# Six instead of four SwiGLU tile pairs from seven products, with each pair's operand sums emitted in the middle of the next pair

## The chip, the cores and the metric

The kernel runs on one core of one Trainium2 chip. The metric is the device time of one execution in microseconds, as a median over runs. The engines are named as the profile names them: PE is TensorE (matmuls), PEld its weight loads, DVE VectorE, ACT ScalarE, POOL GpSimd, SP SyncE, which issues all the DMAs spoken of here.

## What is computed

A decoder block in float32 over 512 tokens of 1024 channels: two token mixers side by side, merged by gates, then a SwiGLU channel mixer with 2816 hidden channels (22 tiles of 128).

```python
D_MODEL, BATCH, SEQ, D_CONV, D_RNN = 1024, 1, 512, 1024, 1280
D_FF = ((int(math.ceil(8 * D_MODEL / 3)) + 255) // 256) * 256      # 2816

h = rmsnorm(x, norm1_g[l])
z = h @ w_in[l] + b_in[l]
z_glu, z_rx, z_rg, z_ga, z_gb = jnp.split(z, split_idx, axis=-1)
...
y_a = u @ conv_w_out[l] + conv_b_out[l]
...
y_b = (hb * jax.nn.gelu(z_rg, approximate=True)) @ lru_w_out[l]
m = jax.nn.sigmoid(z_ga) * y_a + jax.nn.sigmoid(z_gb) * y_b
x = x + m @ w_mix_out[l]

h = rmsnorm(x, norm2_g[l])
x = x + (jax.nn.silu(h @ ffn_w1[l]) * (h @ ffn_w3[l])) @ ffn_w2[l]
return rmsnorm(x, norm_f_g)
```

## The kernel before

**Numbers in two parts.** TensorE multiplies float32 values rounded to a shorter form (F32R), so every factor is held as a high part and the rest, and a product is three matmuls: high by high, high by low, low by high (`mm3` for whole tiles, `Sevenfold.product` for quarters). Making the two parts is a "split": a copy on ACT (L117) and a subtraction (L113) on DVE, or on POOL for the first weights.

**Weights come in blocks.** `wchunk` lists them in the order of use, `emit_chunk` issues one: a DMA of 512 KB into one of four raw buffers (L144, or L242 for the output weights), then the split into one of five hl buffers. `weights` emits four blocks ahead of the one asked for. Blocks carry names: f1_6 is tile 6 of `ffn_w1`, fb11_4 and ft2_4 (here "fb", "ft") blocks for pair 4 from seven products, ob11_2, ob21_2, ot2_0 and so on those of the output weights `ffn_w2`.

**Stages.** TensorE goes through the input product (z), the two mixer outputs (yb with the lo blocks, ya with the co blocks), the mixer's output matrix (mxr), the SwiGLU (f, fr), the last product (or), in this order. An instruction scheduler orders the instructions on each engine by their emission and readiness; some places are fixed by `issue_after`.

**Products of quarters.** A matrix product whose factors are cut into 2x2 quarters can be made with seven quarter products in place of eight, from sums of quarters. `Quartered` and `Sevenfold` do it for `w_mix_out` and `ffn_w2`: `make_sums` loads two 512 KB rows of quarters (ows, L279), makes four sums with four DVE operations of 128x512 and stores them in DRAM as four pieces of 256 KB (ot, L289), from where they are loaded as weights; `Sevenfold.pair` makes the sums of the other factor for one k (ous, s1, s1p, oe, ov); `run` multiplies them, in a first loop over k with the quarters b21 and b11 and the sum t1 (blocks ob21 for two k at a time, and ob11 with b11 and t1 for each k), then in a second.

**The SwiGLU.** The 22 hidden tiles are taken as 11 pairs k = 0 to 10 (tile k and tile k + 11). A direct pair multiplies all of `h2` by the four weight blocks f1 and f3 of its two tiles, with 512 columns a matmul. The pairs in `SEVEN`, 2 to 5, come from `ffn_seven`: seven products r1 to r7 of 256 columns (its seven weight blocks include four sums of quarters), put together in `c11`, `c12`, `c21` and `q`, with `out_of` for the silu and the product with the second factor. The sums of these pairs' weights are made long before, beside the input product: `make_f_sums` is a generator, advanced once for each step of `ORDER` and once for each lo tile; each of its 16 steps loads 4 x 256 columns of `ffn_w1` or `ffn_w3` into a buffer of the pool `wsums` (fws, L334), lets POOL make four sums (128x256) and stores them (fs, L349).

**Order around the change.** After each pair, `out_sums(n)` makes the next n sets of sums of `ffn_w2`: k % 2 after a pair from seven products, two after a direct pair, all that are left after the last. Before, sets 2 and 3 stand after pairs 3 and 5, sets 4 and 5 after pair 6, 6 and 7 after pair 7, 8 and 9 after pair 8, 10 after pair 9. Behind pair 10 come the first blocks of the last product, and the loads of the residual rows x2b and of the final norm's gain gf (`loads`, 10 x 256 KB), which `run` calls after k = 0.

Of the kernel before, what the change touches and what calls it, by code (L numbers as in the profile page):

```python
# [9 lines left out]
F32R = mybir.dt.float32r  # L10
# [3 lines left out]
P = 128  # L14
T = 512
# [25 lines left out]

SEVEN = (2, 3, 4, 5)
SUMS_AT, SUMS_STEP, SUMS_LAG, STORE_LAG = 4, 3, 2, 5


# [33 lines left out]
def tile_block(ctx, tc, a, out):  # L81
    nc = tc.nc
    pool = lambda name, bufs, **k: ctx.enter_context(tc.tile_pool(name=name, bufs=bufs, **k))
    consts = pool("consts", 1)
    raws = pool("raws", RAW)
    hls = pool("hls", HL)
    wsums = pool("wsums", 3)
    psum = pool("psum", 6, space=bass.MemoryType.PSUM)
    psum2 = pool("psum2", 2, space=bass.MemoryType.PSUM)

# [6 lines left out]
    def pairt(name, dtype=F32R):  # L97

        return longt(f"{name}h", dtype), longt(f"{name}l", dtype)

    def bank(name):
        return psum.tile([P, T], F32, tag="mm", name=name)
# [4 lines left out]
    vec, act, pe, pool_e = nc.vector, nc.scalar, nc.tensor, nc.gpsimd  # L107
# [4 lines left out]
    def sub(eng, o, x, y):  # L112
        return eng.tensor_tensor(out=o, in0=x, in1=y, op=ALU.subtract)  # L113

    def split_to(h, l, full, eng, copy=act.copy):

        copy(h, full)  # L117
        last = sub(eng, l, full, h.bitcast(F32))
        if eng is pool_e:
            newest["sub"] = last.ins  # L120
        return h, l

    def split(name, full, eng, p_=None, copy=act.copy):
        p_ = p_ or pairt(name)
        return split_to(*p_, full, eng, copy)
# [4 lines left out]
    emitted = [0]  # L130
# [166 lines left out]
    F_SUMS = ("t2", "t1", "t4", "t3")  # L297
    f_sums = {k: dram.tile([P, 4, 1024], F32, tag=f"fs{k}", name=f"fs{k}") for k in SEVEN}

# [15 lines left out]
    def make_f_sums():  # L315

        todo = [(k, i, c) for k in SEVEN for i in range(2) for c in (0, 2)]
        sums_due, stores_due = [], []  # L320
        n = 0
        while todo or sums_due or stores_due:
            if stores_due and emitted[0] >= stores_due[0][0]:
                stores_due.pop(0)[1]()
            if sums_due and n >= sums_due[0][0]:
                sums_due.pop(0)[1]()
            if todo and n >= SUMS_AT and (n - SUMS_AT) % SUMS_STEP == 0:
                k, i, c = todo.pop(0)
                raw = wsums.tile([P, 1024], F32, tag="wsum", name=f"fws{k}_{i}_{c}")
                q = [raw[:, 256 * m : 256 * m + 256] for m in range(4)]  # L330
                four = (w1, w3)[i].rearrange("p (h k) (e n) -> p h k e n", h=2, e=2)
                with tc.issue_after(newest["load"]):
                    for h in range(2):
                        nc.sync.dma_start(  # L334
                            raw[:, h * T : h * T + T].rearrange("p (e k n) -> p e k n", e=2, k=2),
                            four[:, h, c : c + 2, :, k * P : (k + 1) * P].rearrange("p k e n -> p e k n"),
                        )

                def sums(raw=raw, q=q, k=k, at=T * i + P * c):
                    q11, q12, q21, q22 = q  # L340
                    with tc.issue_after(newest["sub"]):
                        sub(pool_e, q22, q22, q12)
                        sub(pool_e, q12, q12, q11)
                        pool_e.tensor_tensor(out=q11, in0=q22, in1=q11, op=ALU.add)
                        sub(pool_e, q21, q21, q11)

                    def stores():
                        with tc.issue_after(newest["load"]):
                            nc.sync.dma_start(f_sums[k][:, :, at : at + 256], raw.rearrange("p (m n) -> p m n", m=4))  # L349

                    stores_due.append((emitted[0] + STORE_LAG, stores))

                sums_due.append((n + SUMS_LAG, sums))
            n += 1
            yield

    for k in range(KF):
        if k in SEVEN:
            for n in ("b11", "b21", "b22", "t2", "t1", "t3", "t4"):
# [68 lines left out]
    def pc(name, i):  # L428
        return par[:, col[name] + i : col[name] + i + 1]
# [14 lines left out]
    def w_tiles(key, kt, ahead=AHEAD):  # L444
        h, l = weights(key, ahead)
        return [(h[:, k, :], l[:, k, :]) for k in range(kt)]
# [205 lines left out]
    def run_beside(n):  # L652
        for _ in range(n):
            next(side, None)
# [107 lines left out]
    f_sums_steps = make_f_sums()  # L762
# [30 lines left out]
            mixq.make_sums(j // 2 - 1)  # L793
    yb = sgb
    run_beside(1000)
    for _ in f_sums_steps:
        pass


    add = lambda o, x, y: vec.tensor_tensor(out=o, in0=x, in1=y, op=ALU.add)  # L800
# [8 lines left out]

    class Sevenfold:  # L810
        def __init__(self, q):
            self.q, self.uv, self.ops = q, [], []
            self.name, self.kh = q.name, q.kh

        def tile(self, j, make):

            k, i = j % self.kh, j // self.kh
            if i == 0:
                self.uv.append((longt(f"{self.name}u{k}"), longt(f"{self.name}v{k}")))
            for dst, cs in zip(self.uv[k], HALVES):  # L820
                make(cs, dst[:, HALVES[i]])
            if i:
                self.pair(k, *self.uv[k])

        def pair(self, k, ua, va):

            n = self.name
            u_ = split(f"{n}us{k}", ua, vec)
            s1 = shortt(f"{n}s1{k}")[:, LO]
            add(s1, va[:, LO], va[:, HI])  # L830
            sp = longt(f"{n}s1p{k}", F32R)
            split_to(sp[:, LO], sp[:, HI], s1, vec)
            e = longt(f"{n}e{k}")
            sub(vec, e[:, HI], ua[:, LO], va[:, LO])
            sub(vec, va[:, LO], s1, ua[:, LO])
            sub(vec, e[:, LO], ua[:, HI], va[:, LO])
            self.ops.append((u_, sp, e, va))
# [58 lines left out]
    for n, j in enumerate(mixq.order()):  # L896
        ws = w_tiles(f"co{j}", ND)
        ps = bank(f"ya{j}")
        mm3(ps, ws, un)
        o = sga[j]  # L900
        vec.scalar_tensor_tensor(out=o, in0=ps, scalar=pc("conv_b_out", j), in1=o, op0=ALU.add, op1=ALU.mult)
        m7.tile(j, lambda cs, dst: add(dst, o[:, cs], yb[j][:, cs]))
        if n == 0:
            mixq.make_sums(3)


    x2 = [[longt(f"x2{t}{h}") for h in range(2)] for t in range(NT)]
# [48 lines left out]
    o7 = Sevenfold(outq)  # L956
# [54 lines left out]
    def ffn_seven(k):  # L1011
        u_, v_ = longt(f"ou{k}"), longt(f"ov{k}")

        def product(ps, x_, w_, again=False):

            h, l = weights(f"f{w_}_{k}")
            for i in range(2):
                for c, (xh, xl) in enumerate(f_in[x_]):
                    for m, (lw, rx_) in enumerate(((h, xh), (h, xl), (l, xh))):
                        pe.matmul(  # L1020
                            ps[:, HALVES[i]], lw[:, 4 * i + c, :], rx_, start=not (again or i or c or m),
                            stop=bool(i and c == 3 and m == 2), skip_group_check=True,
                        )

        def out_of(c, dst):
            act.activation(c[:, LO], c[:, LO], AF.Silu)
            vec.tensor_tensor(out=dst, in0=c[:, LO], in1=c[:, HI], op=ALU.mult)

        r1, r2, r3, r5, r7 = bank(f"fr1_{k}"), bank2(f"fr2_{k}"), bank(f"fr3_{k}"), bank2(f"fr5_{k}"), bank(f"fr7_{k}")
        product(r1, "a11", "b11")  # L1030
        c11 = shortt(f"c11_{k}")
        act.copy(c11, r1)
        product(r2, "a12", "b21")
        add(c11, r2, c11)
        out_of(c11, u_[:, LO])
        product(r3, "s4", "b22")
        product(r1, "s2", "t2", True)
        q = shortt(f"q_{k}")
        act.copy(q, r1)
        product(r5, "s1", "t1")  # L1040
        add(q, r5, q)
        c12 = shortt(f"c12_{k}")
        add(c12, r3, q)
        out_of(c12, u_[:, HI])
        product(r7, "s3", "t3")
        c21 = shortt(f"c21_{k}")
        act.copy(c21, r7)
        add(q, r7, q)
        out_of(q, v_[:, HI])
        product(r1, "a22", "t4", True)  # L1050
        add(c21, r1, c21)
        out_of(c21, v_[:, LO])
        o7.uv.append((u_, v_))
        o7.pair(k, u_, v_)

    for k in range(1, KF):
        if k in SEVEN:
            ffn_seven(k)
            out_sums(k % 2)
            continue  # L1060
        for j in (k, k + KF):
            p1, p3 = bank(f"f1_{j}"), bank(f"f3_{j}")
            mm3(p1, w_tiles(f"f1_{j}", ND), h2)
            mm3(p3, w_tiles(f"f3_{j}", ND), h2)
            ffn_out(j, p1, p3)
        out_sums(2 if k < KF - 1 else KF)
# [96 lines left out]
```

## Time and profile before

| what | value |
|---|---|
| median of 3 runs | 814.71 us (814.35 to 815.43) |
| the profiled execution, whole | 814.89 us |
| its span | 813.0 us |
| PE busy in the span | 800.0 us |
| DVE / ACT / POOL busy | 644.1 / 443.1 / 210.3 us |
| DMA, moved / mean rate | 153.46 MB / 189 GB/s |
| granted clock of TensorE | 0.995 |

The span is what the profiler recorded from the first instruction to the last; 1.9 us of the profiled execution lie around it. Busy times are sums over instructions of one engine, so they overlap between engines. The names left of an arrow are what an instruction writes, right of it what it reads, with the buffer numbers left out: "f" are the banks of direct pairs, "fr" those of pairs from seven products, "or" those of the last product.

### The profile page before, as it was taken

The page shows a single profiled execution, that of the slowest core. Times are in us where ns is not written, and L with a number is a line of the kernel's source. Part 1 is how long each engine was busy: PE and PEld are TensorE (multiplying, and loading weights), DVE is VectorE, ACT ScalarE, POOL GpSimd, SP SyncE. Part 2 cuts the span into 40 slices and gives each one's busy share as a digit, 9 for nine tenths or more (in the row PEclk, how much of TensorE's full clock was granted, in tenths as well). Part 3 has the DMA queues.
Part 4 walks back from the last instruction along what each step waited for, and adds up shares of the span by engine and source line. Part 5 has one row for each costly group of instructions (what it writes and reads, how often), then busy time and mean ns, then how long its engine had stood idle before and what let it go on. Part 6 is the DMA issues. An engine that isn't in the chain of part 4 may idle for free.

```text
span 813.0 us, 11453 instructions
## 1 busy us (share of the span) xinstructions
PE 800.0 (98%) x4038; PEld 683.3 (84%) x4038; DVE 644.1 (79%) x1010; ACT 443.1 (55%) x626; POOL 210.3 (26%) x156
## 2 busy tenths in 40 slices
PE   8999999999999999999999999999999999999996
PEld 7988888888887888888888898999988888888884
DVE  4699899998999987777878769797875664688456
ACT  7546688776687755653336554364632223476442
POOL 3565768766675740000000042000000000000000
PEclk9999999999999999999999999999999999999998
DMA  6646475666654522358638535788778778576542
GB/s 209 193 123 171 136 202 176 189 193 198 186 170 130 182 75 65 116 171 263 217 104 259 156 97 176 238 262 248 224 247 282 249 271 297 177 250 216 169 160 104
DMA packets 182029, 153.46 MB, mean 189 GB/s; under 512 B 12519, under 2 KB 150163, under 8 KB 181971
## 3 DMA queue, kind: packets, MB, share of 16 engines
q1 hardware_dynamic: 181971, 152.72, 60.7%
q8 instruction: 32, 0.52, 0.3%
q14 instruction: 26, 0.21, 0.1%
HBM read 123.46 MB, written 26.21 MB: 184 GB/s over the span
## 4 chain that ended last, share of the span: by engine, by line
PE 93%; DVE 4%; issue 1%; DMA 1%; SPq 0%; POOL 0%; ACT 0%; POOLq 0%
PE z L441 31%; PE f L441 19%; PE or L844 13%; PE fr L1020 10%; PE yb L441 7%; PE ya L441 5%; PE mxr L844 5%; DVE cv L600 2%; PE g L721 2%; DMA raw_in<-in_w_in_dram 1%; PE th L481 0%; DVE xb L745 0%; PE tx L481 0%; DVE of L1086 0%; SPq L397 0%
## 5 line engine op out<-in xcount | busy, mean ns | idle before, releaser
L600 DVE SCALAR_TENSOR_TENSOR cv<-u,par,cv 128x511 f32<-128x511 f32 (+17 forms) x240 | 162.6, 729 | 1.1 <-ACT cv L597 0.9
L113 POOL TENSOR_TENSOR hl_in<-raw_in,hl_in 128x1024 fp32r<-128x1024 f32 x52 | 125.5, 2418 | 94.0 <-ACT hl_in L117 92.0
L117 ACT CAST hl_in<-raw_in 128x1024 fp32r<-128x1024 f32 x52 | 54.3, 1044 | 5.9 <-PE z L441 3.0
L117 ACT CAST hl_f<-raw_f 128x1024 fp32r<-128x1024 f32 x28 | 29.3, 1050 | 49.1 <-DMA raw_f<-in_ffn_w_dram 36.0
L113 DVE TENSOR_TENSOR hl_ob<-raw_ob,hl_ob 128x1024 fp32r<-128x1024 f32 (+1 forms) x23 | 27.1, 1178 | 26.8 <-ACT hl_ob L117 26.6
L113 DVE TENSOR_TENSOR hl_f<-raw_f,hl_f 128x1024 fp32r<-128x1024 f32 x28 | 36.2, 1304 | 14.3 <-ACT hl_f L117 14.2
L994 POOL TENSOR_TENSOR hf<-h20h,h20l 128x512 f32<-128x512 f32 x1 | 1.3, 1287 | 171.8 <-DVE h20l L485 171.8
L117 ACT CAST hl_ob<-raw_ob 128x1024 fp32r<-128x1024 f32 (+1 forms) x23 | 23.4, 1015 | 40.3 <-PE or L844 17.4
L441 PE MATMUL z<-h10h,hl_in 128*128 128x512 f32 (+1 forms) x112 | 42.4, 380 | 2.7 <-DVE h10l L485 1.5
L441 PE MATMUL z<-h15h,hl_in 128*128 128x512 f32 (+1 forms) x112 | 42.0, 376 | 0.0
L441 PE MATMUL z<-h16h,hl_in 128*128 128x512 f32 (+1 forms) x112 | 42.0, 376 | 0.0
L441 PE MATMUL z<-h17h,hl_in 128*128 128x512 f32 (+1 forms) x112 | 41.9, 376 | 0.0
L441 PE MATMUL z<-h11h,hl_in 128*128 128x512 f32 (+1 forms) x112 | 41.8, 375 | 0.0
L441 PE MATMUL z<-h12h,hl_in 128*128 128x512 f32 (+1 forms) x112 | 41.8, 375 | 0.0
L441 PE MATMUL z<-h14h,hl_in 128*128 128x512 f32 (+1 forms) x112 | 41.8, 375 | 0.0
L441 PE MATMUL z<-h13h,hl_in 128*128 128x512 f32 (+1 forms) x112 | 41.8, 375 | 0.0
L113 POOL TENSOR_TENSOR fws<-fws 128x256 f32<-128x256 f32 x48 | 36.3, 756 | 2.3
L113 DVE TENSOR_TENSOR ows<-ows,ows 128x512 f32<-128x512 f32 x22 | 15.2, 689 | 20.6 <-DMA ows<-in_ffn_w_dram 20.4
L113 DVE TENSOR_TENSOR hl_ot<-raw_ot,hl_ot 128x1024 fp32r<-128x1024 f32 (+1 forms) x17 | 20.1, 1191 | 11.1 <-ACT hl_ot L117 10.7
L441 PEld LDWEIGHTS z<-h10h,hl_in 128*128 128x128 f32 x112 | 21.3, 191 | 7.4 <-DVE h10l L485 1.8
L117 ACT CAST hl_ot<-raw_ot 128x1024 fp32r<-128x1024 f32 (+1 forms) x17 | 17.5, 1028 | 16.5 <-PE or L844 14.8
L441 PEld LDWEIGHTS z<-h15h,hl_in 128*128 128x128 f32 x112 | 21.4, 191 | 3.8
(905 smaller groups left out, 2574.9 us busy)
## 6 DMA issues: line engine op xcount, KB each, us to landing
raw_in<-in_w_in_dram SPq DMA_DIRECT2D x52, 512.0 KB
raw_f<-in_ffn_w_dram SPq DMA_DIRECT2D x28, 512.0 KB
ows<-in_ffn_w_dram SPq DMA_DIRECT2D x22, 512.0 KB
ot<-ows SPq DMA_DIRECT2D x44, 256.0 KB
raw_ob<-in_ffn_w_dram SPq DMA_DIRECT2D x33, 256.0 KB
raw_ot<-ot SPq DMA_DIRECT2D x33, 256.0 KB
fws<-in_ffn_w_dram SPq DMA_DIRECT2D x32, 256.0 KB
fs<-fws SPq DMA_DIRECT2D x16, 512.0 KB
```

Source lines behind the costliest of these rows:

```text
L113: return eng.tensor_tensor(out=o, in0=x, in1=y, op=ALU.subtract)
L117: copy(h, full)
L441: pe.matmul(ps, l, r, start=i == 0, stop=i == n - 1)
L600: vec.scalar_tensor_tensor(out=acc[c][:, s:], in0=u[c][:, : T - s], scalar=dw(c, s), in1=acc[c][:, s:], op0=ALU.mult, op1=ALU.add)
L721: pe.matmul(ps, l, r, start=k == 0, stop=k == len(mms) - 1)
L844: pe.matmul(banks[i], l_[:, ts], r_, start=start and n == 0, stop=stop and n == 2, skip_group_check=again)
L994: pool_e.tensor_tensor(out=v, in0=h2p[c][0].bitcast(F32), in1=h2p[c][1].bitcast(F32), op=ALU.add)
L1020: pe.matmul(ps[:, HALVES[i]], lw[:, 4 * i + c, :], rx_, start=not (again or i or c or m), stop=bool(i and c == 3 and m == 2), skip_group_c ...
```

## The change

`SEVEN` becomes 2 to 7, so two direct pairs (6 and 7) become pairs from seven products. `make_f_sums` therefore has 24 steps; its last ones are now also advanced in the loop over the co tiles and finished after it, and a store is issued as soon as nothing else is left to do.

`Sevenfold.pair` is no longer called at the end of its pair but put on a list, `waiting`. `release` empties the list: in the middle of the next pair from seven products (behind `c12`), where after the last of them (pair 7) one entry is kept; before each direct pair; and in `tile`, at the end of a direct pair. For k = 0, 1 and 2 the split of `u` uses the buffers of `wsums`, free by then, in place of two long tiles.

`out_sums` and its calls are not changed. They now follow other pairs: set 2 after pair 3, 3 after pair 5, 4 after pair 7, 5 and 6 after pair 8, 7 and 8 after pair 9, 9 and 10 after pair 10.

```diff
@@ -41,7 +41,8 @@
-SEVEN = (2, 3, 4, 5)
+PIECES = 3
+SEVEN = (2, 3, 4, 5, 6, 7)
 SUMS_AT, SUMS_STEP, SUMS_LAG, STORE_LAG = 4, 3, 2, 5
@@ -84,7 +85,7 @@
     consts = pool("consts", 1)
     raws = pool("raws", RAW)
     hls = pool("hls", HL)
-    wsums = pool("wsums", 3)
+    wsums = pool("wsums", PIECES)
     psum = pool("psum", 6, space=bass.MemoryType.PSUM)
     psum2 = pool("psum2", 2, space=bass.MemoryType.PSUM)
@@ -320,7 +321,7 @@
         sums_due, stores_due = [], []
         n = 0
         while todo or sums_due or stores_due:
-            if stores_due and emitted[0] >= stores_due[0][0]:
+            if stores_due and (emitted[0] >= stores_due[0][0] or not (todo or sums_due)):
                 stores_due.pop(0)[1]()
             if sums_due and n >= sums_due[0][0]:
                 sums_due.pop(0)[1]()
@@ -793,8 +794,6 @@
             mixq.make_sums(j // 2 - 1)
     yb = sgb
     run_beside(1000)
-    for _ in f_sums_steps:
-        pass
     add = lambda o, x, y: vec.tensor_tensor(out=o, in0=x, in1=y, op=ALU.add)
@@ -809,7 +808,7 @@
     class Sevenfold:
         def __init__(self, q):
-            self.q, self.uv, self.ops = q, [], []
+            self.q, self.uv, self.ops, self.waiting = q, [], [], []
             self.name, self.kh = q.name, q.kh
         def tile(self, j, make):
@@ -820,12 +819,23 @@
             for dst, cs in zip(self.uv[k], HALVES):
                 make(cs, dst[:, HALVES[i]])
             if i:
-                self.pair(k, *self.uv[k])
+                self.waiting.append((k, *self.uv[k]))
+                self.release()
+        def release(self, keep=0):
+            while len(self.waiting) > keep:
+                self.pair(*self.waiting.pop(0))
         def pair(self, k, ua, va):
             n = self.name
-            u_ = split(f"{n}us{k}", ua, vec)
+            p_ = None
+            if n == "o" and k < PIECES:
+                both = wsums.tile([P, 1024], F32R, tag="wsum", name=f"{n}us{k}")
+                p_ = both[:, :T], both[:, T:]
+            u_ = split(f"{n}us{k}", ua, vec, p_)
             s1 = shortt(f"{n}s1{k}")[:, LO]
             add(s1, va[:, LO], va[:, HI])
             sp = longt(f"{n}s1p{k}", F32R)
@@ -902,6 +912,10 @@
         m7.tile(j, lambda cs, dst: add(dst, o[:, cs], yb[j][:, cs]))
         if n == 0:
             mixq.make_sums(3)
+        next(f_sums_steps, None)
+    for _ in f_sums_steps:
+        pass
     x2 = [[longt(f"x2{t}{h}") for h in range(2)] for t in range(NT)]
@@ -1042,6 +1056,8 @@
         c12 = shortt(f"c12_{k}")
         add(c12, r3, q)
         out_of(c12, u_[:, HI])
+        o7.release(1 if k == SEVEN[-1] and len(SEVEN) > 5 else 0)
         product(r7, "s3", "t3")
         c21 = shortt(f"c21_{k}")
         act.copy(c21, r7)
@@ -1051,13 +1067,14 @@
         add(c21, r1, c21)
         out_of(c21, v_[:, LO])
         o7.uv.append((u_, v_))
-        o7.pair(k, u_, v_)
+        o7.waiting.append((k, u_, v_))
     for k in range(1, KF):
         if k in SEVEN:
             ffn_seven(k)
             out_sums(k % 2)
             continue
+        o7.release()
         for j in (k, k + KF):
             p1, p3 = bank(f"f1_{j}"), bank(f"f3_{j}")
             mm3(p1, w_tiles(f"f1_{j}", ND), h2)
```

## The prediction

> **What bounds the kernel now.** I read the page's busy shares first, then its chain that ended last, then that chain in order of time.
>
> ```profile
> span 813.0 us, 11453 instructions
> PE 800.0 (98%) x4038; PEld 683.3 (84%) x4038; DVE 644.1 (79%) x1010; ACT 443.1 (55%) x626; POOL 210.3 (26%) x156
> PE z L441 31%; PE f L441 19%; PE or L844 13%; PE fr L1020 10%; PE yb L441 7%; PE ya L441 5%; PE mxr L844 5%; DVE cv L600 2%; PE g L721 2%; DMA raw_in<-in_w_in_dram 1%; PE th L481 0%; DVE xb L745 0%; PE tx L481 0%; DVE of L1086 0%; SPq L397 0%
> ```
>
> ```profile
> 480.34 30.60 PE f L441 x169
> 510.94 80.63 PE fr L1020 x672
> 591.57 108.83 PE f L441 x480
> 700.40 102.93 PE or L844 x453
> ```
>
> The second fence is start, length and instructions of each link. TensorE alone carries the end, from 480 to 803 us without a gap. So a removed matmul is worth its spacing, and a late weight block costs its lateness. The link "fr" is the four pairs from seven products, the 108.83 us after it the five direct pairs (6 to 10), "or" the output product, whose first loop takes 18 matmuls for each of 11 k.
>
> The windows (bounds, length, busy us of PE, PEld, DVE, ACT, POOL, clock, DMA share, GB/s) give the room beside it:
>
> ```profile
> 314.00:380.00 66.00, 66.00 (x292) 54.64 (x291) 51.36 (x73) 36.53 (x55) 0.00 (x0) 1.00 0.48 152
> 531.00:551.00 20.00, 20.00 (x169) 20.00 (x169) 17.51 (x27) 13.01 (x20) 0.00 (x0) 1.00 0.83 249
> 657.00:679.00 22.00, 22.00 (x99) 18.23 (x98) 13.06 (x23) 6.40 (x9) 0.00 (x0) 1.00 0.85 280
> 679.00:700.00 21.00, 21.00 (x94) 17.39 (x93) 10.25 (x16) 5.73 (x8) 0.00 (x0) 1.00 0.61 212
> ```
>
> Even a seven-product pair leaves DVE 2.5 us of 20. The last direct pair (679 to 700) is the quiet one, DMA share 0.61: in it the kernel finishes loading for "or".
>
> **What is removed.** A direct pair is 96 matmuls of 512 columns at 108.83 / 480 = 226.7 ns: 21.77 us. A seven-product pair is 672 / 4 = 168 matmuls of 256 columns at 80.63 / 672 = 120.0 ns: 20.16 us. Two pairs change over: 2 x 1.61 = 3.22 us less TensorE.
>
> A rule that speaks against it: the Trainium skill, "TensorE: Matmul & The Clock Gate", section "Back-to-back issue gap", says that in a stream the weight load and the matmul together set the spacing, so short matmuls lose, and gives about 81 ns at 128 and 131 ns at 512 columns. Interpolated (an estimate from that page), 256 columns at 98 ns would make the seven products 3.9 us dearer per pair. The rows, 120.0 and 226.7 ns, differ from both figures, and they decide.
>
> **What is added, at nothing.** Eight more steps of sums in the middle of the program: 16 loads of 256 KB, 8 stores of 512 KB, and 8 x 4 = 32 POOL subtractions or additions of 128x256. POOL is idle there (0.00 of 66 us above), at 0.74 to 0.756 us each they take 24 us of it. The DMA share is 0.48. Two things could show through. A DVE split beside POOL is slower:
>
> ```profile
> L113 DVE TENSOR_TENSOR hl_f<-raw_f,hl_f 128x1024 fp32r<-128x1024 f32 x28 | 36.2, 1304 | 14.3 <-ACT hl_f L117 14.2
> L113 POOL TENSOR_TENSOR fws<-fws 128x256 f32<-128x256 f32 x48 | 36.3, 756 | 2.3
> L113 DVE TENSOR_TENSOR hl_ob<-raw_ob,hl_ob 128x1024 fp32r<-128x1024 f32 x21 | 25.7, 1224 | 24.4 <-ACT hl_ob L117 24.2 <-DMA x2b<-x2k 0.2
> ```
>
> (busy us and mean ns after the bar; hl_ob never meets POOL, a few of hl_f do and take 1.8 us instead of 1.22). At worst each of the 32 costs DVE 0.6 us: 19 us, against 66.00 - 51.36 = 14.6 us of idle DVE in this window and 9.8 in the next 44 us. And a load of such a step can hold SP until an earlier store has landed (16.9 us over 6 loads before, 5.3 at most), with the weight loads of "yb" behind it; these were ready 4.7 us or more before their use. I take 0; with that cover gone, 5.3 - 4.7 = 0.6 us each time.
>
> The seven products need seven 512 KB blocks a pair instead of four, and seven splits. Pairs 2 to 5 did that without a gap, with DVE at 17.51 of 20: 0. The smallest margin there, from split to use, was 0.9 us, in pair 2, whose order is unchanged; in pair 4, which makes sums of the last weights (ows) as well, it fell from 8.8 to 3.3; in pair 5 it grew to 6.8. Pair 6 is a second pair 4, pair 7 a second pair 5.
>
> The moved sums of each pair are some 3 us of DVE (subtractions of 0.42 and 0.69 us). Nothing on TensorE reads them before "or"; they only leave the place where the next pair's splits wait. 0, and 3 us of DVE if that room were gone. Three of the splits using the wsums buffers cost nothing either.
>
> **What is moved without being named.** The sums of the last weights are made one for each odd seven-product pair, two for each direct pair, the rest at the end. Before, k = 10 had none left: sums 8 and 9 stood in pair 8, 10 in pair 9. With two direct pairs less, sums 9 and 10 fall behind pair 10, the quiet one. The built order of the queues says so: on SP, the loads of ows9 and ows10 and their eight stores stand among the first loads of "or" (before raw_ob11_2), and the last two pieces of block ob11_4 stand on both sides of ten other loads (x2b and gf, 2.5 MB); on DVE, ows10's four operations and pair 10's sums stand before the split of hl_ob11_2. On TensorE ob21_4's 12 matmuls go ahead of ob11_4's; nothing else changes there. This I cost with rows of pair 8, where two sets also stood:
>
> ```profile
> 661.84 0.69 DVE L113 TENSOR_TENSOR ows<-ows,ows 128x512 f32<-128x512 f32 x1 [2.97 <-DMA ows<-in_ffn_w_dram]
> ...
> 666.56 0.69 DVE L113 TENSOR_TENSOR ows<-ows,ows 128x512 f32<-128x512 f32 x1
> 667.16 2.36 DVE L113 TENSOR_TENSOR hl_f<-raw_f,hl_f 128x1024 fp32r<-128x1024 f32 x2
> ```
>
> ```profile
> 691.90 5.76 SPq L242 DMA_DIRECT2D raw_ob<-in_ffn_w_dram  x3
> 697.71 0.43 SPq L242 DMA_DIRECT2D raw_ob<-ot  x1
> 702.82 0.33 SPq L242 DMA_DIRECT2D raw_ob<-in_ffn_w_dram  x1
> 703.19 0.43 SPq L242 DMA_DIRECT2D raw_ob<-ot  x1
> 703.72 3.70 SPq L1076 DMA_DIRECT2D x2b<-x2k  x8
> 708.31 0.33 SPq L1078 DMA_DIRECT2D gfh<-in_norm_f_g_dram  x1
> ```
>
> All in before's times (after, everything here is 3.22 earlier). TensorE needs hl_ob11_2 at 700.40 + 2 x 18 x 0.2267 = 708.56. Two ends for it. Pair 10 as pair 8, two pairs of 21.77 later: ows10's operations end at 667.25 + 43.53 = 710.8, the split (1.22) at 712.0: 3.4 us late. Followed wait by wait: the load of ows10's second half needs the buffer that hl_ob21_2's split frees at about 700.4, 512 KB land 3.3 us later on the emptier queue, 703.7; the operations and pair 10's sums, 5 us on DVE, end at 708.7 to 709.1; the split at 709.9 to 710.3: 1.3 to 1.7 late. I take 1.6, as the DMA share here is that of 679 to 700 and not pair 8's 0.85.
>
> Then ob11_4. Its buffer comes free with hl_ob11_2's, so its first piece is issued at about 710.8, x2b00 at 711.25. After eight loads in flight SP pauses until the oldest has landed (707.4 to 708.31 above); the second piece is the eleventh and issues at 716.0 to 717.1. The 2.5 MB take 0.67 us for each 256 KB, so it lands 721.2 to 722.5; its cast (1.05) ends 722.25 to 723.55. TensorE comes there 2 x 4.08 + 12 x 0.2267 = 10.9 us after hl_ob11_2's split, at 720.8 to 721.1: 1.5 to 2.8 late, and 0.35 more for its split. I take 2.4. Later blocks were ready 4.0 to 5.6 us early and their loads are delayed no further: 0.
>
> **Sum.** -3.22 + 1.6 + 2.4 = +0.8, with ends of -3.22 + 1.3 + 1.85 = -0.1 and -3.22 + 3.4 + 3.15 = +3.3. The profiled execution took 814.89 us (813.0 of span and 1.9 around it), 0.18 above the median 814.71. So 815.7 by it, 815.5 by the median.
>
> **Rivals.** 0.2% (1.6 us, about what a measurement tells from no change) puts "same" at 813.1 to 816.3.
>
> - The gain is kept: the sums fit into the quiet pair. For it: DMA share 0.61, DVE 10.25 of 21 us, and blocks ready 12 to 18 us early there. Against: hl_ob11_2 itself had only 5.6 us. Without any stall 814.71 - 3.22 = 811.5; with up to half the price, 813.1. Chance 0.24.
> - Slower: the queue at the start of "or" runs as pair 8 did. From a lateness of hl_ob11_2 above 2.4 us it decides: 3.4 and 3.15 us lost give 814.71 + 3.3 = 818.0. For it: SP's order is fixed, so one late store holds every load behind it. Against: the lower DMA share. Chance 0.25.
> - Slower: the longer run of seven-product pairs drains its margin. If pairs 6 and 7 each lost the 5.5 us that pair 4 lost, 6.8 - 11 = -4.2: 4.2 us more, 819.7. Against: pair 5 recovered 3.5. Chance 0.06.
> - Slower in the middle: POOL holds up DVE. At 0.6 us for 32 operations, 19 us against some 24 of idle DVE up to 424; only if they bunch does it show, 1 to 3 us: 816.5 to 818.5. Chance 0.03. The Trainium skill, "SBUF — State Buffer", section "Who interferes with whom", has the harder rule that a two-input DVE operation and a POOL operation reading SBUF exclude each other for the whole instruction. By that, an estimate, 24 us instead of 19; the 1.8 us splits agree in kind.
>
> The forecast itself, 813.1 to 816.3, has 0.42. So faster 0.24, same 0.42, slower 0.34; its own range is 814.6 to 816.3, and 811.4 to 818.2 leaves out some 2 in 10, the drained margin and a little on each side.
>
> **What would show it.** Right: "fr" at 6 x 20.16 = 121.0 us with 1008 matmuls, "f" after it 65.3 us with 288, no gap before 697; then gaps of 1 to 3.4 us before the matmuls of hl_ob11_2 and of hl_ob11_4, with ACT or DVE hl_ob as releasers behind ows and x2b. Wrong: "or" at 102.9 us (gain kept), a gap inside "fr" or "yb", or spacings other than 120.0 and 226.7 ns.

## The result, and the profile after

The changed kernel takes 819.81 us (median of 6 runs, 818.07 to 821.0); the kernel before, with the runs made beside it, 814.26 (813.72 to 815.43). The ratio is 1.0065, 95% interval 1.0051 to 1.0079: slower, and above the predicted range. The profiled execution took 819.45 us.

The span is 817.7 us, 4.7 longer than before. What differs is how long TensorE needs for each stage (first start to last end of its matmuls, read from both traces):

| stage | before, us | after, us |
|---|---|---|
| yb and ya | 98.56 | 98.57 |
| f and fr | 463.19 to 700.40, 237.2 | 463.32 to 697.36, 234.0 |
| of it fr | 80.8 (672 matmuls) | 121.1 (1008) |
| or | 700.24 to 805.36, 105.1 | 697.19 to 810.89, 113.7 |

So the products give 3.2 us, as worked out, and the last product gives back 8.6. The first lines of the changed kernel's page, and its windows (columns as before), show where:

```profile
span 817.7 us, 11871 instructions
PE 800.2 (98%) x4182; PEld 688.7 (84%) x4182; DVE 663.0 (81%) x1026; ACT 452.6 (55%) x642; POOL 243.1 (30%) x188
```

```profile
697.20:705.50 8.30, 8.30 (x37) 6.57 (x35) 5.28 (x10) 1.24 (x2) 0.00 (x0) 1.00 0.90 311
705.50:710.00 4.50, 0.76 (x3) 0.43 (x3) 3.73 (x7) 2.72 (x5) 0.00 (x0) 0.80 0.53 202
710.00:715.00 5.00, 5.00 (x12) 3.93 (x13) 2.04 (x3) 0.35 (x1) 0.00 (x0) 0.50 0.76 263
715.00:722.00 7.00, 7.00 (x32) 5.75 (x31) 4.55 (x7) 3.93 (x7) 0.00 (x0) 1.00 1.01 341
722.00:726.00 4.00, 2.79 (x12) 1.69 (x11) 2.16 (x3) 2.53 (x4) 0.00 (x0) 1.00 1.01 382
```

Read down: TensorE works until about 705.5, then has 0.76 us of work in 4.5; from 710 to 715 it is busy but fits 12 matmuls into 5 us, at a granted clock of 0.50; then it is itself again until 722, and waits a second time. The matmuls' own timeline says for what (start, length of the group, and in brackets the idle time before it and what ended it):

```profile
705.98 0.50 PE L854 MATMUL or<-hl_ob,ous 128*128 128x512 f32 x1 [0.47 <-ACT hl_ob L118]
709.75 5.06 PE L854 MATMUL or<-hl_ob,ous 128*128 128x512 f32 x11 [3.27 <-DVE hl_ob L114]
```

From each step between two matmul starts, 0.227 us is taken off as the matmul's own; the rest is lost: 0.63 and 3.55 us at hl_ob11_2, 2.56 over twelve steps behind it, most of them 427 ns long, and 1.76 at hl_ob11_4. That is 8.5 of the 8.6 us.

Why hl_ob11_2 is so late stands on SP (first fence) and DVE (second):

```profile
688.31 4.62 SPq L280 DMA_DIRECT2D ows<-in_ffn_w_dram  x3
699.31 0.33 SPq L280 DMA_DIRECT2D ows<-in_ffn_w_dram  x1
703.44 5.47 SPq L290 DMA_DIRECT2D ot<-ows  x4
709.76 1.28 SPq L243 DMA_DIRECT2D raw_ob<-in_ffn_w_dram  x3
711.16 4.53 SPq L1093 DMA_DIRECT2D x2b<-x2k  x8
717.24 0.33 SPq L243 DMA_DIRECT2D raw_ob<-ot  x1
```

```profile
695.28 0.69 DVE L114 TENSOR_TENSOR ows<-ows,ows 128x512 f32<-128x512 f32 x1 [2.70 <-DMA ows<-in_ffn_w_dram]
698.07 1.22 DVE L114 TENSOR_TENSOR hl_ob<-raw_ob,hl_ob 128x1024 fp32r<-128x1024 f32 x1
...
702.72 0.69 DVE L114 TENSOR_TENSOR ows<-ows,ows 128x512 f32<-128x512 f32 x1 [2.78 <-issue]
...
706.27 0.42 DVE L114 TENSOR_TENSOR os1p<-os,os1p 128x256 fp32r<-128x256 f32 x1 [0.98 <-ACT os1p L118]
...
708.49 2.35 DVE L114 TENSOR_TENSOR hl_ob<-raw_ob,hl_ob 128x1024 fp32r<-128x1024 f32 x2
```

The second half of ows9, issued at 688.73, landed at 695.15, the last of 2 MB queued since 686.45. Its operations end at 698.2, hl_ob21_2's split behind them frees a raw buffer at 699.3, and only then the second half of ows10 is loaded. Its operations and pair 10's sums hold DVE from 702.7; in the middle DVE idles 0.98 us for a copy of os1p that ACT makes only after the cast of hl_ob11_2, whose last piece landed at 704.78. The split of hl_ob11_2 ends at 709.7. Meanwhile SP stands 5.5 us in set 10's four stores, which wait for those operations, so that ob21_4, ob11_4's first piece, x2b and ob11_4's second piece (717.24, landed 723.21) follow late.

The chain that ended last goes the same way. It has no TensorE in it from 699.28 us, where it begins, to 725.59 (start, length; short links left out at the dots):

```profile
700.17 4.61 DMA raw_ob<-ot
704.88 1.05 ACT hl_ob L118
...
708.57 1.15 DVE hl_ob L114
...
712.05 5.18 DMA x2b<-x2k
717.24 5.97 DMA raw_ob<-ot
...
725.59 83.27 PE or L854 x365
```

So block ob11_4 sets the end of "or", and hl_ob11_2 takes part by the raw buffer that its split frees late.

### The profile page after: what moved, and what is told of

It reads as the page before. It is cut to its first block, busy times and chain, and to the rows that moved or that the text cites. A ratio compares the mean times of both kernels' runs of the same rounds, so it can differ in the third digit from the quotient of the medians.

```text
span 817.7 us, 11871 instructions
## 1 busy us (share of the span) xinstructions
PE 800.2 (98%) x4182; PEld 688.7 (84%) x4182; DVE 663.0 (81%) x1026; ACT 452.6 (55%) x642; POOL 243.1 (30%) x188
## 5 line engine op out<-in xcount | busy, mean ns | idle before, releaser
L114 POOL TENSOR_TENSOR fws<-fws 128x256 f32<-128x256 f32 x72 | 62.2, 867 | 74.0 <-DMA fws<-in_ffn_w_dram 70.8
L114 DVE TENSOR_TENSOR hl_ft<-raw_ft,hl_ft 128x1024 fp32r<-128x1024 f32 x24 | 29.2, 1219 | 8.9 <-ACT hl_ft L118 8.8
L1034 PE MATMUL fr<-hs_0h,hl_ft 128*128 128x256 f32 x192 | 35.5, 283 | 0.0
L118 ACT CAST hl_f<-raw_f 128x1024 fp32r<-128x1024 f32 x20 | 20.9, 1048 | 26.0 <-PE f L442 11.3
L118 ACT CAST hl_ft<-raw_ft 128x1024 fp32r<-128x1024 f32 x24 | 24.9, 1048 | 17.6 <-DMA raw_ft<-fs 15.9
L114 DVE TENSOR_TENSOR hl_f<-raw_f,hl_f 128x1024 fp32r<-128x1024 f32 x20 | 26.6, 1336 | 7.7 <-ACT hl_f L118 7.6
L1034 PEld LDWEIGHTS fr<-hs_0h,hl_ft 128*128 128x128 f32 x192 | 30.4, 192 | 0.0
L114 DVE TENSOR_TENSOR hl_fb<-raw_fb,hl_fb 128x1024 fp32r<-128x1024 f32 x18 | 23.1, 1282 | 7.3 <-ACT hl_fb L118 7.2
```

Of the source, the lines that this page charges most:

```text
L1034: pe.matmul(ps[:, HALVES[i]], lw[:, 4 * i + c, :], rx_, start=not (again or i or c or m), stop=bool(i and c == 3 and m == 2), skip_group_c ...
```

## The experiments

All are the changed kernel with one edit unless said otherwise. Times are medians; ratios are to the kernel before, timed beside each.

**Two sets behind pair 10, or something else?** One set after each seven-product pair leaves none for the end:

```diff
-            out_sums(k % 2)
+            out_sums(1)
```

> The changed kernel, with one set of sums of ffn_w2 after each of the six seven-product pairs (in place of after every second), so that sets 8 and 9 follow pair 8, 10 follows pair 9 and none pair 10, as in the kernel before. Theory (the whole loss comes from the two sets left behind pair 10, the seven-product pairs themselves keep their 3.2 us): the stage of the last product takes 105 us again instead of 113.7, no gap before hl_ob11_2 or hl_ob11_4, 810.8 to 811.5 us, 0.4% faster than before. Rival (the longer run of seven-product pairs has no room, and the tight 0.5 us margin of pair 2 shows it): three more sets of 2.8 us on DVE and 2 MB of transfers in pairs 2, 4 and 6 open gaps inside fr, and the time is 814 or more.

821.49 us, 1.0089 (1.0075 to 1.0103). Theory and rival both hold, each for its stage: "or" takes 105.1 us again, without a gap; but f and fr take 244.6 us instead of 234.0. The gaps are in the seven-product pairs, in the window of pair 5 for instance, where the kernel before had no idle TensorE:

```profile
571.40:595.00 23.60, 20.51 (x155) 19.90 (x154) 17.51 (x26) 11.44 (x17) 0.00 (x0) 0.93 0.82 257
```

DVE is at 17.5 of 23.6 us, so it isn't full. Four of the gaps (0.4, 2.0, 0.6 and 1.6 us) stand between the blocks b22 and t2 of a pair and end with ACT's copy c11, which must read bank r1 before t2 may add to it. For the longest, at 582.5, that copy stood on ACT behind the cast of hl_ft1_5, for which ACT had idled 2.75 us, since its load (landed 582.79) was issued on SP behind the two loads of a set, which hold two of four raw buffers.

**The same lateness without the six pairs.** The kernel before, with its sets made later:

```diff
-        out_sums(2 if k < KF - 1 else KF)
+        out_sums({6: 0, 7: 1}.get(k, 2) if k < KF - 1 else KF)
```

> The kernel before with its four seven-product pairs, and the sets of sums of ffn_w2 made as late as in the changed kernel: none after pair 6, one after 7, two after 8 and 9, sets 9 and 10 after pair 10. Theory (this place alone makes the loss): the last product's stage is 8 to 9 us longer than before, 822 to 823.5 us, 1.0 to 1.1% slower. Rival (the loss needs the six seven-product pairs or the deferred sums too): within 2 us of before, 814 to 816.5.

820.18 us, 1.0072 (1.0058 to 1.0085); "or" 111.3 us. The place alone makes a loss as large as the whole result, but the stage lost 6.2 us and not 8 to 9. TensorE does not wait for hl_ob11_2 here. It waits 0.87 us for DVE's last product of pair 10 and 3.15 us at hl_ob11_4, and loses some 1.6 us in slow matmuls behind that. The two traces tell why it is less: the split of hl_ob11_2 ends at 708.8 here and at 709.7 in the changed kernel, hl_ob11_4's first matmul comes at 723.0 and at 724.3, though "or" begins at 699.8 here and at 697.2 there. In these two traces the queue of loads, sums and splits runs at its own pace, not TensorE's: a TensorE that arrives 2.6 us earlier waits longer.

**The second wait.** The x2b and gf loads are called after k = 5 of the last product:

```diff
-                if k == 0:
+                if k == 5:
                     begun()
```

> The changed kernel, with the ten loads of x2b and gf called after k = 5 of the last product in place of k = 0; on SP they then stand behind ob11_9. Theory (the second wait, 1.7 us before hl_ob11_4, is due to these 2.5 MB between the two pieces of that block): that wait goes, the first wait and the slow matmuls behind it stay, 818.1 us. Rival (ob11_4 is late since its raw buffer comes late): the second wait stays above 1 us, 819.8.

816.90 us, 1.0032 (1.0019 to 1.0045). The wait at hl_ob11_4 is gone and the first one stays (0.57 and 3.55 us). The size isn't settled: in the profile "or" is only 0.8 us shorter (112.9), as the ten loads now make 2.0 us of gaps around ot2_0, and 1.7 us of the difference lie in the input product, which no edit touches.

**The slow matmuls.** Sixteen matmuls that nobody reads, ahead of those of hl_ob11_2:

```diff
+                if n == "o" and k == 2:
+                    fill = bank2("fill")
+                    for _ in range(16):
+                        pe.matmul(fill, u_[0][:, :P], u_[0], start=True, stop=True)
```

> The changed kernel, with 16 matmuls of 512 columns that nobody reads on TensorE ahead of the products of hl_ob11_2 (3.6 us of work in the place of the 4.1 us wait), nothing else added. In the changed kernel 12 matmuls after that wait come 427 ns apart instead of 227, at a granted clock of 0.69. Theory (the clock was lowered because TensorE stood idle for over 3 us): all matmuls after it come 227 ns apart, and the time falls by 2.5 us to 817.3. Rival (the matmuls are slow because weights or transfers around them are late, or the clock answers to something else): they stay at 427 ns and the time is 819.8 or a little more.

822.04 us, 1.0090 (1.0076 to 1.0103): the theory had the time wrong, and the slow matmuls right. TensorE's timeline of this run:

```profile
704.92 3.79 PE L872 MATMUL fill<-ous 128*128 128x512 f32 x16
...
709.27 2.81 PE L854 MATMUL or<-hl_ob,ous 128*128 128x512 f32 x11 [0.34 <-DVE hl_ob L114]
...
723.38 1.22 PE L854 MATMUL or<-hl_ob,ous4h 128*128 128x512 f32 x2 [4.50 <-ACT hl_ob L118]
724.40 1.05 PE L854 MATMUL or<-hl_ob,os1p 128*128 128x512 f32 x2
```

Behind the filled wait eleven matmuls take 2.81 us, 227 ns apart, where they took 5.06. TensorE then comes to hl_ob11_4 so much earlier, waits 4.5 us there, and the slow matmuls come after that wait. hl_ob11_4's first matmul comes 26.6 us after the start of "or", in the changed kernel 27.1: it bounds the stage in both, and the first wait and the slow matmuls behind it were hidden in the second. Without waits it would come 4 x 4.08 + 2.72 = 19.0 us after the start.

> fill and x2late in one: the 16 unread matmuls ahead of the products of hl_ob11_2, and the x2b loads called after k = 5. In x2late six matmuls after the first wait came 427 ns apart, 1.4 us in all; in fill the slow matmuls moved to the second wait, which grew to 4.5 us. Theory (a wait of 3 us or more lowers TensorE's clock, and unread matmuls keep it up): no slow matmuls at all, a gap under 1 us before hl_ob11_2, 1 to 1.5 us less than x2late: 815.4 to 816. Rival (the slow matmuls go with late weights, not with the idle time): as x2late or slower, 816.9 or more, with 427 ns spacings left.

Both edits at once gave 818.41 us, 1.0060 (1.0042 to 1.0078), slower than x2late, as the rival has it: the time does not decide. The profiled execution was the longest of the six (822.34 us). In it the x2b loads stand ahead of ob11_8, which opens gaps of 1.4 and 1.0 us there with one matmul between, and seven matmuls at 427 ns behind them. Around hl_ob11_2, with a gap of 0.87 us, none is slow.

**What the deferral is worth.** The four pairs of before with the deferred sums (`SEVEN = (2, 3, 4, 5)`), and the six pairs without the deferral:

```diff
         o7.waiting.append((k, u_, v_))
+        o7.release()
```

> The changed kernel with SEVEN = (2, 3, 4, 5): four seven-product pairs as before, only the pairs' sums emitted in the middle of the next pair and three splits in wsums buffers. Theory (nothing on TensorE waits for these sums): same as before within 0.1%, 813.8 to 815.4. Rival (moving the sums changes the order in which splits and sums reach DVE, and so opens or closes gaps): 1 us or more to either side.

> The changed kernel with each seven-product pair's sums emitted at the end of their own pair, as before; TensorE's order is unchanged. Theory (the deferral is worth nothing): as the changed kernel, 819 to 821. Rival (the deferral is what keeps the longer run of pairs free of gaps): gaps in fr, 821 or more.

defer4: 814.64 us, 1.0000 (0.9991 to 1.0009). nodefer: 819.09 us, 1.0062 (1.0049 to 1.0076), f and fr 234.0 us, "or" 113.1. Moving the sums does nothing, with four pairs or with six.

**Half the dose.** Two sets after pair 7, so that one stays for the end:

```diff
+            out_sums(2 if k == 7 else k % 2)
```

> The changed kernel with two sets after pair 7 (4 and 5) in place of one, so that only set 10 is left behind pair 10; in the built order the x2b loads then stand behind ob11_5 again. Theory (half of the cause gives well under half of the loss, since the quiet pair 10 has room for one set): a gap of 0 to 2 us before hl_ob11_2, the last product's stage 105 to 107.5 us, 811.3 to 813.5 us. Rival (any set behind pair 10 costs its own share): half of 8.5 us, 815.5.

814.59 us (eleven runs, 812.79 to 818.53), 1.0009 (0.9997 to 1.0021), no difference from before, and 5.2 us less than with two sets. In the two traces "or" makes only 3.6 us of this: it takes 110.1 us, and the input product, which the edit does not touch, ends 1.6 us earlier. There are waits of 3.0 us at the beginning of "or" and 1.8 at hl_ob11_6. The first ends with DVE's last product of pair 10, which frees a bank and stands on DVE behind set 10's operations. Neither number was right. By the stage, the one set costs 5.0 us, more than half of the two sets' 8.6, which is nearer the rival.

**Sets made earlier.** Sets 0 to 2 in the stages ya and mxr:

```diff
+        if n in (3, 6):
+            outq.make_sums(n // 3 - 1)
...
-    m7.run(x2, lambda: None, mix_end)
+    m7.run(x2, lambda: outq.make_sums(2), mix_end)
...
-    sums_of = iter(range(KF))
+    sums_of = iter(range(3, KF))
```

> The changed kernel, with sets 0, 1 and 2 of the sums of ffn_w2 made in the stages ya (behind co tiles 3 and 6) and mxr; the later sets move up by three, so that two stand after pairs 8 and 9 and none after pair 10. The seven-product pairs have as many sets as in the changed kernel. Theory (nothing but the two sets behind pair 10 is wrong): the last product's stage takes 105 us, fr is unchanged, and 811.0 to 812.0 us follow if ya and mxr have room. Rival (the early sets delay the weight blocks of ya and mxr, DVE idle 9.8 of 44 and 11 of 51 us there, less the sums of quarters of ffn_w1 that already run late): gaps of 2 to 6 us in ya or mxr, 813.5 to 817.5.

816.97 us, 1.0033 (1.0021 to 1.0046). "or" 105.1 and fr 121.1 us, both free of gaps; mxr is 47.3 us instead of 40.0. TensorE waits 1.0 and 2.6 us at its start, for DVE's products of ya behind the early sums, and its next matmuls come 427 ns apart. The early sets had no free place there, as the rival has it.

**Buffers of their own.** The rows for the sums in the `wsums` buffers:

```diff
-            q = [raws.tile([P, 1024], F32, tag="raw", name=f"{self.name}ws{k}_{i}") for i in range(2)]
+            own = self.name == "o"
+            q = [(wsums if own else raws).tile([P, 1024], F32, tag="wsum" if own else "raw", name=f"{self.name}ws{k}_{i}") for i in range(2)]
...
-            if n == "o" and k < PIECES:
+            if False:
```

> The changed kernel, with the rows of ffn_w2 for the sums loaded into the three wsums buffers (free in this stage) in place of the four raw buffers that the weight blocks share, and all splits of u in long tiles again. In the built order the ten sets then run ahead as buffers come free: set 10 is stored before the first block of the last product is loaded, though the calls stand where they did. Theory (in sums1 the seven-product pairs stopped because two of four raw buffers were held by the sums for some 7 us, and in the changed kernel the sets behind pair 10 are late for the same reason): no gap in fr, none at hl_ob11_2 or hl_ob11_4, the last product's stage 105 us, 811.0 to 811.8 us, 0.4% faster than before. Rival (what stops fr is DVE's or SP's order, the added 2.8 us of DVE and eight more entries a pair on SP): gaps in fr of 3 us or more, 814 to 821 us.

817.76 us, 1.0043 (1.0030 to 1.0056). "or" is 105.1 us; fr is 127.8, all of the excess in one place of pair 2, where TensorE waits 2.2 and 1.6 us for the split of hs_1, a sum of quarters of h2, behind sets that ran ahead, and takes 213 ns for a matmul of 256 columns for some us behind it. The later seven-product pairs, with a set each, have no gap: raw buffers, not the work on DVE or SP, were what they lacked in sums1. The calls stand as in the changed kernel, but set 10's last operation ends at 656.8 us, where it ended at 708.6: with buffers of their own the sets are not late. So the sets are to be paced: as after_own from set 2 on, and queued behind their own pair,

```diff
+        newest["pair"] = add(c21, r1, c21).ins
...
-        with tc.issue_after(turned):
+        with tc.issue_after(newest.get("pair", turned)):
```

once with one set after each seven-product pair, once with sets after pairs 3, 5, 6 and 7, two after pair 8 and three after pair 9:

> The changed kernel, with one set of sums of ffn_w2 after each seven-product pair, loaded into the wsums buffers from set 2 on, and its DVE operations queued behind the last addition of its own pair (after_own ran all sets ahead at once and lost 4 us in pair 2 alone). Sets 9 and 10 are then stored beside the first two blocks of the last product. Theory (seven-product pairs have room for one set each, when it holds no raw buffer and is spread evenly): no gap in fr, the last product's stage near 105 us, 811 to 812 us, 0.35% faster than before. Rival (a set more in every pair fills DVE, 17.5 + 2.8 of 20.2 us, and SP with eight more entries a pair): gaps in fr of 3 to 8 us, 815 to 820.

> As paced, with sets after pairs 3, 5, 6 and 7 alone (2 to 5), two after pair 8, three after pair 9, all in wsums buffers. Sets 9 and 10 stand among the first loads of the last product again, but their loads wait for no raw buffer, and the x2b loads stand behind ob11_5. If the late sets hurt by holding raw buffers: the last product's stage 105 to 106.5 us, 811.5 to 813. If they hurt by SP's order and DVE's alone: a gap of 3 us or more before hl_ob11_2, 815 to 819.

paced: 811.10 us, 0.9961 (0.9949 to 0.9973). paced_b: 809.95 us, 0.9949 (0.9936 to 0.9962), faster than both kernels. Its chain has no gap from fr to the end of "or":

```profile
509.92 120.95 PE fr L1035 x1008
630.88 65.31 PE f L443 x288
696.18 102.95 PE or L855 x453
```

In the order of SP, sets 9 and 10 stand among the first loads of "or" in paced_b too. But they are called one pair earlier, behind pair 9, and wait for no raw buffer: set 10's last operation ends at 688.8 us, before "or" begins (696.0). So the run shows that such sets are not late, and not what late sets without raw buffers would cost. Its trace is 5.1 us shorter than that of the kernel before: 3.2 us lie in f and fr, the input product ends 1.0 us earlier, and the time behind "or" is 0.9 us shorter. The last two no edit here was meant to change.

## Why the prediction was wrong, by its steps

- **What is removed** was right: 1008 matmuls in 121.1 us are 120.2 ns each, and f with fr is 3.2 us shorter. The spacing figures of the Trainium skill ("TensorE: Matmul & The Clock Gate", "Back-to-back issue gap") would have had the pairs lose; at full clock the rows held in every run here.
- **What is added, at nothing** was right: yb and ya take 98.57 us as before (98.56), and the fr stage has no gap. The room was smaller than the margins said: three sets more, in raw buffers, cost 10.6 us there (sums1). The 0.6 us "at worst" for a split beside POOL was no bound: it comes from 1.8 us, the mean of four splits of hl_f that took 1.56 to 2.23.
- **The moved sums** at 0: shown by defer4 and nodefer.
- **What is moved without being named** had the right place, blocks and releasers, and the wrong sizes. The failing step is "I take 1.6, as the DMA share here is that of 679 to 700 and not pair 8's 0.85". The share was 0.76 from 686 to 697.2 and 0.90 after it, as the two sets had come into the quiet pair and filled it; the row of the kernel before described a place that the change itself altered. Put in the changed kernel's times (3.22 earlier), the wait-by-wait count has ows10's buffer free at 697.2 and hl_ob11_2 split by 706.7 to 707.1; measured are 699.3 and 709.7. 2.1 us of that is the buffer: hl_ob21_2's split, which frees it, stood behind the operations on ows9, whose second half took 6.4 us to land and not the 3.3 that the count gives a load of this size. Most of the rest is DVE's 0.98 us of idle time for os1p's copy, which stands on ACT behind the late cast and was left out. So hl_ob11_2 cost 4.2 us, beyond even the end from pair 8's rows (3.4).
- **The second wait** was set at 2.4 us and measured 1.8. That these are near is luck: ob11_4's second piece was to land by 719.3 at the latest, in the changed kernel's times, and landed at 723.21, and TensorE came later too, held by the first wait and the slow matmuls.
- **A term was missing**: after the 3.3 us wait twelve matmul steps cost 2.6 us more.
- **The frame "after, everything here is 3.22 earlier"** was wrong too, as before_late shows: the queue into "or" did not move with TensorE, so the gain ended in its wait. With 4.2, 2.6 and 1.8 in place of 1.6 and 2.4 the sum is -3.2 + 8.6 = 5.4 us, beside a measured 819.81 - 814.26 = 5.55. The three were read from the trace of this result, so the sum only shows that nothing else was lost.
- **The rivals**: the slower one, "the queue at the start of 'or' runs as pair 8 did", came nearest: it has 3.4 and 3.15 us lost and 818.0, measured are 4.2 and 1.8, and 2.6 of slow matmuls that it doesn't have. The other three did not occur.

Open: how the waits share the loss (they overlap, as fill shows), and why the input product ends at 323.5 to 326.1 us in these runs; the share of x2late that is its own can't be told for that reason.

## What to carry to other kernels

When work that is tied to loop steps (here the sums of the next weights) is scheduled by counting them, changing the kind of steps moves its tail: count where the last of it ends before pricing anything else. A stage that is quiet now is no row for the cost of work that will move into it; price it by the busy stage that already does that work. A queue that holds a shared buffer while it waits delays whoever shares it; a buffer of its own, with the work paced, made the same sums free.

## What the runs showed of the hardware that was not expected

TensorE can halve its pace after a wait: 427 instead of 227 ns for 512 columns, for some 3 to 7 us, at a granted clock of 0.50 (710 to 715). It followed single idle times of 2.0 us in sums1, 3.0 in before_late, 3.2 to 3.3 in nodefer, x2late and here, and 4.5 in fill, and pairs of shorter ones with one to three matmuls between (0.9 and 2.4 us in early3, 1.3 and 0.8 in fill_x2late, 2.1 and 1.4 in after_own). It did not follow single ones of 0.6 to 1.45 us near 258 us in any run, 2.2 in nodefer, nor 2.85 in one_left.

The length of the wait does not sort these, but the granted clock in the traces does. In each trace it changes only on a grid of steps of 3.41 us, which lies elsewhere against the program in every run. Between 20 and 800 us all nine halvings follow a step in which TensorE was busy for 1.65 us or less; no step at full clock with 1.8 us or more is followed by one:

| run | step, us | TensorE busy in it, us | granted clock in the next step |
|---|---|---|---|
| after | 704.79 to 708.20 | 1.23 | 0.50 |
| sums1 | 582.74 to 586.15 | 1.41 | 0.50 |
| fill_x2late | 737.50 to 740.91 | 1.65 | 0.50 |
| sums1 | 627.11 to 630.52 | 1.81 | 1.00 |
| one_left | 697.32 to 700.73 | 1.86 | 1.00 |
| one_left | 700.73 to 704.15 | 2.13 | 1.00 |

The 2.85 us of one_left lay across two steps, with enough work in each; the 2.0 us of sums1 lay within one. The Trainium skill, "TensorE: Matmul & The Clock Gate", section "Part 1: The HAM clock gate (the "warmup" mystery)", tells of a free-running window of some 3.4 us after which an idle array is clocked at half. The halving and the length of the window agree. That the window need not be idle, with up to 1.65 us of work in it, is measured here.
